# Eight column groups instead of six in the k-blocked opening of a two-layer trunk, and two groups of branch B and C moved in the order

## The chip, the core and the metric

The kernel runs on one core of one Trainium2 chip. The metric is device time in microseconds (us) for one execution of the whole program, both layers. The core has a matmul engine (PE, with its weight loads shown as PEld), a vector engine (DVE), a scalar engine (ACT), GpSimd (POOL) and SyncE (SP), which here issues most of the DMA transfers.

## The reference

384 tokens (128 of a prompt and 256 of a latent grid) of width 2048 go through two layers. Each layer is one input projection, three branches side by side, one output projection and a layer norm:

```
u    = x * (1 + scale) + shift                 # scale, shift, gate = silu(c) @ w_ada + b_ada
proj = u @ w_in                                # 2048 -> 8976 columns, float32
A: RWKV-7 scan, both directions, 8 heads x 64  (conv of r, k, v; decay and a from a LoRA; gate)
B: mLSTM, both directions, 4 heads x 128       (conv of q, k; v, o, i, f; gate)
C: differential attention, 8 heads             (q, k, v; gate)
x    = layer_norm(ALPHA * x + gate * (concat(A, B, C) @ w_out))
```

`w_in` is 2048 x 8976 and `w_ada` 2048 x 6144 for each layer. Context keys, values and final states of the prompt are outputs too.

## The kernel before

**Products.** Every float32 operand of the projections is split in two parts, `hi` (by ACT) and `lo` (by DVE, one in four by POOL). A product of 128 rows of k, 128 columns and 384 tokens is three matmuls. The 16 tiles of k, the two halves of 256 columns and the three matmuls make 96 matmuls for a *column group*, the unit of the order below.

**The opening.** A layer's first groups can't wait for all of `u`. `gemm_head` takes `GROUPS[l]` column groups by blocks of k: in the first layer there are `BLOCKS[0] = 8` blocks of two k tiles. For each block and group it makes 12 matmuls, and the partial result goes from PSUM into an SBUF tile (`part`): ACT copies it in block 0, DVE adds it (`add`) in blocks 1 to 7. After the last block a group's own evacuation runs (for branch A's r, k and v: a convolution, `a_rkv`). The tiles are borrowed from tags that branch A uses later (`HEAD`). In the first layer the same stretch also makes scale and shift: `first0` strews the loads and small matmuls of `w_ada` (eight loads of 512 KB for each block) among the groups, and turns `x` round on PE. Order of the groups: LoRA, k (two groups), r (two), v (first); the second v group follows as an ordinary group (`gemm_ch`, loads of 512 KB, the sum stays in PSUM).

**The main part.** `layer_plan` writes the order of the groups out by hand: after the opening the rest of v, then for C's pairs of heads v, q, k and a gate (`c_pair`, `c_gate`), then `MIX` (a letter for each group: c for C's last v, q and k; q for B's query and key groups; v for B's value groups), then B's gates, C's last gate, A's gates, and the output projection. Branches are generators ("streams"): between two chunks of dense matmuls `pump` lets a few segments of the ready streams in, by a planner's own clocks. So dense groups are the cover under which the thin, chained work of the branches runs. Where an order demands that a branch be over, `drain` writes out all that is left of it with no dense work between:

- `b_first` (before B's first q group) drains A's front stage "AF", since `QK` takes the tile `big0` that it reads.
- `to_b` (before B's first v group) drains all of A and "post"; `a_end` is A's last part (group norm, then the bonus term).
- `c_qk` drains the pair of C heads before, when the next pair's q is evacuated (`self.drain(f"C{h // 2 - 1}")`).
- `b_start` (after B's last v group) starts `b_main`. Its heads wait until all eight q and k tiles are there (`bqk < 8`).
- `o_rest` (after six loads of the output projection) drains everything.

The order is fixed when the program is built; each engine then works through its own list in order.

Of the kernel before, what the change touches and what calls it, by code (L numbers as in the profile page):

```python
# [21 lines left out]
T = 384  # L22
# [11 lines left out]
O_CQ, O_CK, O_CV, O_CGATE = 4880, 5904, 6928, 7952  # L34
# [3 lines left out]
RAWB = 3  # L38
CUTB = 4
LOADS = 6  # L40
GROUPS = (6, 6)
TWO = 100.0, 0.0
ADA = ((0.0, 1.0), (0.0, 1.0))
WARM, DENSE = 3100.0, 2.0
# [5 lines left out]
CPOOL = 4  # L50
PESHARE = 2000.0, 2000.0
HEAD = ("PG", 2), ("QHt", 2), ("Tt", 2), ("BK", 1), ("QH", 1), ("UV", 1), ("ce00", 1), ("ce10", 1)
MIX = "cccqqqvvvvq", "cccqqqvvvvq"
PRIO = {"E": -1, "R": 0, "N": 0, "U": -1, "X": 0, "C": 0, "A": 0, "AI": 0, "AF": 0}
AHEAD = 700.0, 500.0
LAT = 130.0
# [146 lines left out]
class Hybrid:  # L203
# [604 lines left out]
    def gemm_head(self, wv, groups, nb):  # L808

        part = {}  # L810
        bk, hb = KT // nb, KB // 2

        def place():
            for tag, n in HEAD + ((("ce01", 1), ("ce11", 1)) if self.first else (("GE", 2),)):
                for _ in range(n):
                    t = self.ct([128, T], tag) if tag[0] == "c" else self.mt([128, T], tag, bufs=2 if n > 1 else 1)
                    part[len(part) // 2, len(part) % 2] = t

        def add(g, j, kb, o, evac):
            t = part[g, j]  # L820
            if kb == 0:
                self.nc.scalar.copy(t, o)
                return
            self.nc.vector.tensor_tensor(t, o, t, OP.add)
            if kb == nb - 1:
                yield
                yield from evac(j, t)

        def chunk(g, kb, h, hv, lv, evac):
            if g == kb == h == 0:  # L830
                place()
            if h == 0:
                part["ps"] = [self.acc() for _ in range(2)]
            for kk in range(hb):
                kt = kb * bk + h * hb + kk
                self.need_u(kt)
                st, sp = (h == 0 and kk == 0), (h * hb + kk == bk - 1)
                for j in range(2):
                    c = slice(j * 128, j * 128 + 128)
                    o = part["ps"][j][:, 0:T]  # L840
                    self.nc.tensor.matmul(o, hv[:, kk, c], self.uh[:, kt, :], start=st, stop=False)
                    self.nc.tensor.matmul(o, hv[:, kk, c], self.ul[:, kt, :], start=False, stop=False)
                    self.nc.tensor.matmul(o, lv[:, kk, c], self.uh[:, kt, :], start=False, stop=sp)
                    if sp:
                        self.evacuate(add(g, j, kb, o, evac), part["ps"][j])
                self.pump()

        return [[Step("w", lambda h, hv, lv, g=g, kb=kb, evac=evac: chunk(g, kb, h, hv, lv, evac),
                      lambda kb=kb, c0=c0: wv()[:, kb * bk:kb * bk + bk, c0:c0 + 256], 256, bk // hb)
                 for g, (c0, evac) in enumerate(groups)] for kb in range(nb)]  # L850
# [875 lines left out]
    def layer_plan(self, l, first):  # L1726
# [14 lines left out]
        def ch(c0, f, i0, *korder):  # L1741
            return self.gemm_ch(wi, c0, lambda j, s: f(i0 + j, s), *korder)

        cols = [(O_LORA, self.a_lora, 0)] + [(128 * i, self.a_rkv, i) for i in (4, 6, 0, 2, 8, 10)]
        n = GROUPS[l]
        gemm = self.gemm_head(wi, [(c0, lambda j, s, f=f, i=i: f(i + j, s)) for c0, f, i in cols[:n]], BLOCKS[l])
        head = first(gemm, call(begin))
        main = sum((ch(*x) for x in cols[n:]), [])
        self.nhead = n
        v0 = self.gemm_t(wi, O_CV, 256, lambda tb, s: self.c_v(0, tb, s))  # L1750
        main += v0
# [1 line left out]
        def c_pair(pr):  # L1753
            return [self.gemm_t(wi, O_CV + 256 * pr, 256, lambda tb, s: self.c_v(pr, tb, s)),
                    ch(O_CQ + 256 * pr, lambda h, s: self.c_qk(h, 0, s), 2 * pr),
                    ch(O_CK + 256 * pr, lambda h, s: self.c_qk(h, 1, s), 2 * pr) + call(self.c_start, pr)]

        for pr in range(3):
            main += sum(c_pair(pr)[1 if pr == 0 else 0:], []) + ch(O_CGATE + 256 * pr, self.c_gate, 2 * pr)

        def to_b():
            self.drain("A", "post")
# [6 lines left out]
        vs = [self.gemm_t(wi, O_BV + 260 * g, 260, lambda tb, s, g=g: self.b_vo(g, tb, s)) for g in range(4)]  # L1769
        vs[0][0:0] = call(to_b)  # L1770
        vs[3] += call(b_start)
        qs = [ch(O_BQK + 128 * i, self.b_qk, i) for i in range(0, 8, 2)]
        qs[0][0:0] = call(self.b_first)
        parts = {"c": c_pair(3), "v": vs, "q": qs}
        for x in MIX[l]:
            main += parts[x].pop(0)
        for p in (0, 2):
            main += ch(O_BGATE + 128 * p, self.b_gate, p)
        main += ch(O_CGATE + 256 * 3, self.c_gate, 6)
        korder = (2, 0, 3, 1)  # L1780
        for p in (0, 2):
            main += ch(O_AGATE + 128 * p, self.a_gate, p, (0, 1, 2, 3) if p == 0 else korder)
# [8 lines left out]
        else:  # L1791
# [18 lines left out]
            main = main[:at] + tail  # L1810
# [10 lines left out]
        n = sum(1 for st in main if st.kind == "w") - 32  # L1821
# [183 lines left out]
    def run(self):  # L2005
# [51 lines left out]
        plan = self.layer_plan(0, first0)  # L2057
        self.early = 64 + BLOCKS[0] * GROUPS[0] - GROUPS[0]
        for l in range(1, DEPTH):
# [39 lines left out]
```

## Time and profile before

| | |
|---|---|
| median of 3 runs | 2265.77 us (2263.94 to 2270.36) |
| the profiled execution, its own time | 2266.75 us |
| span of its trace | 2265.0 us |
| PE busy | 2160.2 us (95%) |
| mean granted clock of PE | 0.979 |

The profile is of one execution. Its own time is 1.75 us more than its span (what lies before the first and after the last instruction), and 0.98 us more than the median. A clock of 1.00 is 2.4 GHz, 0.50 is 1.2 GHz. Every instruction bears line 156, that of the helper which records it, so rows are told apart by their tiles: `acc` is the PSUM of the projections, `ada` that of `w_ada`, `mx` that of the branches; `cq` and `ck` are C's queries and keys, `big` is `big0` and its kind. Ends of matmuls are modelled, so a matmul that is listed with 0.34 us may start 0.18 us behind the one before.

### The profile page before, as it was taken

The numbers are of one execution on the slowest core, as the hardware profiler recorded it, in microseconds if no ns is written. First come the engines' busy times: TensorE is split into PE (matmuls) and PEld (weight loads), VectorE is DVE, ScalarE is ACT, GpSimd is POOL, SyncE is SP. The second block draws the span as 40 slices with busy tenths as digits, with TensorE's granted clock in tenths as the row PEclk, the third lists the DMA queues.
The fourth block names the chain that finished last, engine by engine and source line by source line (L and its number), as shares of the span: only waits on it lengthen the run. The fifth ranks groups of instructions, "written<-read, shape, count | busy, mean of one in ns | idle before, by whom it ended". The sixth has DMA issues, their size and how long they took to land.

```text
span 2265.0 us, 45639 instructions
## 1 busy us (share of the span) xinstructions
PE 2160.2 (95%) x17629; PEld 1903.1 (84%) x17629; DVE 1409.5 (62%) x3792; ACT 950.1 (42%) x2207; POOL 664.6 (29%) x894
## 2 busy tenths in 40 slices
PE   5999999999999999999998999999989999999998
PEld 3778878777787888889998998788878888999997
DVE  1667776766765633577338677777676754367634
ACT  2345344343343433444327443434334443344543
POOL 3111333423332211112436123352433320111344
PEclk9999999999999999999999999999999998999998
DMA  9995433433434465544465432232222323434444
GB/s 317 314 317 145 148 114 106 120 105 108 129 115 126 151 186 162 168 145 150 152 219 176 127 115 76 83 97 82 82 82 78 92 86 113 122 103 120 144 142 144
DMA packets 313794, 314.90 MB, mean 139 GB/s; under 512 B 17569, under 2 KB 309030, under 8 KB 313450
## 3 DMA queue, kind: packets, MB, share of 16 engines
q1 hardware_dynamic: 305450, 299.49, 43.5%
q0 software_dynamic: 3616, 10.22, 1.3%
q8 instruction: 139, 2.28, 0.4%
q10 hardware_dynamic: 4512, 2.28, 0.3%
q14 instruction: 77, 0.63, 0.1%
HBM read 298.83 MB, written 13.12 MB: 138 GB/s over the span
## 4 chain that ended last, share of the span: by engine, by line
PE 69%; DVE 15%; DMA 5%; ACT 4%; issue 4%; POOL 2%; SPq 1%; DVEq 0%; ACTq 0%; POOLq 0%
PE acc L156 50%; PE mx L156 16%; DMA raw<-in_w_in_dram 3%; PE ada L156 3%; DVE lo L156 3%; ACT hi L156 2%; DVE mixed L156 2%; DVE big L156 1%; DVE GE L156 1%; POOL crs L156 1%; DVE tm L156 1%; POOL lo L156 1%; DVE BK L156 1%; DVE cmx L156 1%; DVE Di L156 1%
## 5 line engine op out<-in xcount | busy, mean ns | idle before, releaser
L156 PE MATMUL acc<-uh,hi 128*128 128x384 f32 x2240 | 809.1, 361 | 14.1 <-ACT hi L156 7.4
L156 PE MATMUL acc<-uh,lo 128*128 128x384 f32 x2240 | 763.4, 341 | 2.3 <-DVE lo L156 0.8
L156 PE MATMUL acc<-ul,hi 128*128 128x384 f32 x2240 | 762.9, 341 | 1.7 <-DVE ul L156 1.7
L156 DVE TENSOR_TENSOR lo<-raw,hi 128x512 fp32r<-128x512 f32 (+1 forms) x496 | 361.3, 739 | 494.7 <-ACT hi L156 478.0
L156 ACT CAST hi<-raw 128x512 fp32r<-128x512 f32 (+1 forms) x659 | 395.6, 619 | 427.0 <-PE acc L156 274.0
L156 POOL TENSOR_TENSOR lo<-raw,hi 128x512 fp32r<-128x512 f32 (+1 forms) x163 | 222.6, 1366 | 998.3 <-ACT hi L156 914.4
L156 PEld LDWEIGHTS acc<-uh,hi 128*128 128x128 f32 x2240 | 426.5, 190 | 75.9 <-issue 29.7
L156 PEld LDWEIGHTS acc<-ul,hi 128*128 128x128 f32 x2240 | 426.6, 190 | 6.1 <-DVE ul L156 3.3
L156 PEld LDWEIGHTS acc<-uh,lo 128*128 128x128 f32 x2240 | 425.2, 190 | 6.9 <-DVE lo L156 5.5
L156 PE MATMUL acc<-hi,uh 128*128 128x256 f32 (+1 forms) x768 | 227.8, 297 | 4.0 <-DVE mixed L156 1.7
L156 PE MATMUL acc<-lo,uh 128*128 128x256 f32 (+1 forms) x768 | 218.0, 284 | 1.1 <-DVE lo L156 1.0
L156 PE MATMUL acc<-hi,ul 128*128 128x256 f32 (+1 forms) x768 | 217.1, 283 | 0.0
L156 PEld LDWEIGHTS acc<-hi,uh 128*128 128x128 f32 x768 | 145.8, 190 | 22.8 <-issue 12.3
L156 PEld LDWEIGHTS acc<-lo,uh 128*128 128x128 f32 x768 | 145.9, 190 | 2.3 <-DVE lo L156 2.3
L156 PEld LDWEIGHTS acc<-hi,ul 128*128 128x128 f32 x768 | 145.9, 190 | 0.0
L156 ACT ACTIVATE ce<-mx,cmx 128x384 f32<-128x384 f32 (+1 forms) x96 | 48.0, 505 | 109.0 <-DVE cmx L156 109.0
L156 PE MATMUL ada<-raw,sil 128*32 128x256 f32 x1088 | 87.9, 398 | 4.3 <-DMA raw<-in_w_ada_dram 4.3
L156 ACT COPY mixed<-mx 64x256 f32<-64x256 f32 x120 | 44.0, 366 | 101.8 <-PE mx L156 99.9
L156 PEld LDWEIGHTS mx<-mixed 128*64 128x64 f32 x1536 | 54.1, 141 | 24.8 <-issue 9.1
L156 PE MATMUL mx<-mixed 128*64 128x64 f32 x1536 | 67.5, 232 | 3.7 <-DVE mixed L156 2.4
L156 DVE TENSOR_TENSOR mixed<-mx,mixed 128x256 f32<-128x256 f32 (+1 forms) x96 | 40.1, 418 | 34.3 <-PE mx L156 33.9
L156 POOL TENSOR_TENSOR GE<-th,big 64x512 f32<-64x512 f32 x24 | 33.0, 1375 | 81.6 <-PE mx L156 69.6
(449 smaller groups left out, 3074.2 us busy)
## 6 DMA issues: line engine op xcount, KB each, us to landing
raw<-in_w_in_dram SPq DMA_DIRECT2D x224, 512.0 KB
raw<-in_w_ada_dram SPq DMA_DIRECT2D x136, 512.0 KB
raw<-in_w_out_dram SPq DMA_DIRECT2D x64, 512.0 KB
big<-in_w_ada_dram SPq DMA_DIRECT2D x42, 512.0 KB
raw<-in_w_in_dram SPq DMA_DIRECT2D x32, 520.0 KB
GE<-in_w_ada_dram SPq DMA_DIRECT2D x14, 512.0 KB
cq<-xs SPq DMA_DIRECT2D x32, 192.0 KB
big<-in_w_in_dram SPq DMA_DIRECT2D x21, 256.0 KB
```

Source lines behind the costliest of these rows:

```text
L156: r = f(*args, **kw)
```

## The change

The first layer's opening takes eight groups: the second v group of A and C's third gate (`c_gate` of heads 4 and 5) come in, with four more SBUF tiles (`hx`). Both then leave the main part of the first layer. In both layers B's fourth q group moves from behind B's v groups to before them, and C's last gate moves from behind B's gates to right behind B's v groups. The last block's order of groups is LoRA, k, k, r, r, v, v, gate.

```
-GROUPS = (6, 6)
+GROUPS = (8, 6)
-MIX = "cccqqqvvvvq", "cccqqqvvvvq"
+MIX = "cccqqqqvvvvg", "cccqqqqvvvvg"
...
-            for tag, n in HEAD + ((("ce01", 1), ("ce11", 1)) if self.first else (("GE", 2),)):
+            for tag, n in HEAD + ((("ce01", 1), ("ce11", 1), ("hx", 4)) if self.first else (("GE", 2),)):
                 for _ in range(n):
-                    t = self.ct([128, T], tag) if tag[0] == "c" else self.mt([128, T], tag, bufs=2 if n > 1 else 1)
+                    t = self.ct([128, T], tag) if tag[0] == "c" else self.mt([128, T], tag, bufs=n)
...
+        cols += [(O_CGATE + 512, self.c_gate, 4)]
...
-        main = sum((ch(*x) for x in cols[n:]), [])
+        main = sum((ch(*x) for x in cols[n:7]), [])
...
-            main += sum(c_pair(pr)[1 if pr == 0 else 0:], []) + ch(O_CGATE + 256 * pr, self.c_gate, 2 * pr)
+            main += sum(c_pair(pr)[1 if pr == 0 else 0:], [])
+            if pr < 2 or n < 8:
+                main += ch(O_CGATE + 256 * pr, self.c_gate, 2 * pr)
...
-        parts = {"c": c_pair(3), "v": vs, "q": qs}
+        parts = {"c": c_pair(3), "v": vs, "q": qs, "g": [ch(O_CGATE + 256 * 3, self.c_gate, 6)]}
...
-        main += ch(O_CGATE + 256 * 3, self.c_gate, 6)
```

Counted in dense groups, the order of the first layer is then: after the opening 1 + 3 + 4 + 3 + 3 = 14 groups up to `b_first` (16 before), four more up to `to_b` (three before), so 18 in place of 19 between the opening and `to_b`. In the second layer it is 16 up to `b_first` as before, and 20 in place of 19 up to `to_b`. In both layers five groups follow `b_start` before the output projection, where there were six.

## Rows read from the trace of the kernel before

**Rows 1.** The page: busy time of the engines, share of the span, instructions.
```profile
PE 2160.2 (95%) x17629; PEld 1903.1 (84%) x17629; DVE 1409.5 (62%) x3792; ACT 950.1 (42%) x2207; POOL 664.6 (29%) x894
```

**Rows 2.** Windows over the opening: us; PE, PEld, DVE, ACT, POOL busy; PEclk; DMA; GB/s.
```profile
30.00:40.00 10.00, 6.54 (x38) 4.89 (x40) 3.09 (x6) 4.08 (x9) 1.38 (x3) 0.69 1.08 363
40.00:50.00 10.00, 8.92 (x85) 5.84 (x80) 3.24 (x7) 4.66 (x11) 1.28 (x1) 0.97 1.01 336
50.00:60.00 10.00, 9.39 (x73) 6.98 (x70) 3.91 (x8) 7.68 (x17) 1.28 (x1) 1.00 0.95 318
...
170.00:180.00 10.00, 10.00 (x59) 10.00 (x58) 8.83 (x19) 6.04 (x11) 3.49 (x5) 1.00 0.67 185
180.00:190.00 10.00, 7.94 (x31) 6.37 (x29) 8.56 (x20) 4.25 (x8) 0.76 (x2) 0.83 0.37 109
...
60.00:160.00 100.00, 100.00 (x766) 77.32 (x759) 63.36 (x144) 37.42 (x75) 15.95 (x18) 1.00 0.97 324
```

**Rows 3.** Timeline of PE in the opening: start us, us, operation, count, idle before.
```profile
99.18 0.34 PE L156 MATMUL acc<-uh,hi 128*128 128x384 f32 x1
...
100.59 0.34 PE L156 MATMUL acc<-uh,lo 128*128 128x384 f32 x1
100.86 0.64 PE L156 MATMUL ada<-big,sil 128*32 128x256 f32 x8
101.43 0.44 PE L156 MATMUL acc<-uh,hi 128*128 128x384 f32 x1
```

**Rows 4.** Timeline of PE at the opening's end.
```profile
183.43 1.11 PE L156 MATMUL mx<-gt,const 128*128 128x384 f32 x2 [1.25 <-ACT gt L156]
```

**Rows 5.** Timeline of PE at the end of branch A, second layer.
```profile
1875.50 0.91 PE L156 MATMUL mx<-PG,const 128*128 128x384 f32 x2
1880.19 0.33 PE L156 MATMUL mx<-q,big 64*64 64x64 f32 x2 [3.78 <-DVE q L156]
```

**Rows 6.** Windows there, columns as in rows 2.
```profile
1875.00:1880.00 5.00, 1.41 (x10) 0.38 (x10) 4.86 (x13) 3.23 (x6) 1.28 (x1) 1.00 0.59 159
1880.00:1885.00 5.00, 4.12 (x36) 3.60 (x36) 2.98 (x9) 4.85 (x7) 0.00 (x0) 0.54 0.17 58
1885.00:1890.00 5.00, 4.99 (x58) 4.99 (x59) 4.63 (x8) 0.00 (x0) 0.00 (x0) 0.50 0.00 0
1890.00:1895.00 5.00, 5.00 (x29) 4.88 (x28) 1.57 (x5) 0.50 (x1) 0.00 (x0) 0.59 0.35 105
```

**Rows 7.** Timeline of PE at the end of branch A, first layer.
```profile
734.65 0.91 PE L156 MATMUL mx<-PG,const 128*128 128x384 f32 x2
...
779.13 0.33 PE L156 MATMUL mx<-q,big 64*64 64x64 f32 x2
```

**Rows 8.** Timeline of ACT around C's third pair, first layer.
```profile
586.97 0.29 ACT L156 COPY ck<-acc 128x128 f32<-128x128 f32 x1
...
686.52 0.37 ACT L156 COPY rraw<-acc 128x256 f32<-128x256 f32 x1 [3.82 <-PE acc L156]
```

**Rows 9.** Timeline of PE there.
```profile
668.88 1.03 PE L156 MATMUL mx<-const,cq 128*128 128x128 f32 x3 [1.03 <-POOL cq L156]
...
677.82 1.00 PE L156 MATMUL mx<-const,QH 64*128 64x64 f32 x8
```

**Rows 10.** Timeline of PE in branch B, first layer, then second.
```profile
902.62 0.53 PE L156 MATMUL mx<-const,PG 4*128 4x4 f32 x6
...
918.83 0.71 PE L156 MATMUL mx<-const,big 128*128 128x128 f32 x3
...
1065.15 0.49 PE L156 MATMUL mx<-const,big 128*128 128x128 f32 x3
...
1981.66 0.53 PE L156 MATMUL mx<-const,PG 4*128 4x4 f32 x6
...
1994.86 0.75 PE L156 MATMUL mx<-const,big 128*128 128x128 f32 x4
...
2121.82 0.49 PE L156 MATMUL mx<-const,big 128*128 128x128 f32 x3
```

## The prediction, made before the changed kernel was run

> **What bounds the kernel now.** I read the page first: PE is busy for 95% of the span, PE's weight loads for 84%, and no other engine for more than 62% [rows 1]. The change removes no matmul and adds none. So it can only win back time in which PE waits or runs at its lower clock (2266.75 us hold about 105 us of idle PE, 2265.0 less 2160.2), or lose some. The question is where that time lies, and whether a place that the change touches has it.
>
> Next I read windows over the opening, where DMA is busiest: there one would look for a PE that starves. PE is short of work up to about 60 us: idle 3.46 us from 30 to 40, 1.08 from 40 to 50, 0.61 from 50 to 60. From 60 to 160 us it is busy 100.00 of 100 us, with DMA at 0.97 [rows 2]. Since busy time is modelled, I checked with PE's timeline that no wait hides in it: nine products in a row start within 1.41 us of each other, 0.176 us apart, the `ada` matmuls of a load follow 0.27 us behind the last of them, and the next product starts 0.57 us later, with no wait named [rows 3]. Both resources are near full here, and PE is the one that has no gap. At the opening's end PE is idle for 2.06 us, most of it in a wait of 1.25 us for ACT's `gt`, which stands behind a queue of convolutions, and its clock falls to 0.83 for 10 us [rows 2, 4].
>
> Then I went through PE's timeline for waits over 3 us in the places where the order changes. One stands out: in the second layer `a_end` is not over when `to_b` drains it. The last matmul on `PG` starts at 1875.50, and the next one 4.69 us later, having waited 3.78 us for DVE; the bonus matmuls follow bare, at a clock of 0.54, 0.50 and 0.59 [rows 5, 6]. The same piece of the first layer (from the `PG` matmul at 734.65 to the last `q` at 779.13) runs under dense groups without a wait [rows 7].
>
> **The opening, its size.** Two groups of eight blocks move in. A block of a group is 12 matmuls at 0.176 us [rows 3], 2.11 us; 7 blocks x 2 x 2.11 = 29.6 us of PE work before the last block and 4.2 us in it, all of which leaves the main part. Where PE is already full this is neutral: same work, other place. It only pays where PE waits for lack of work after the first product could start. That is 40 to 60 us: 1.08 + 0.61 = 1.69 us at most [rows 2]; the 3.46 us before it lie ahead of the first product, which the number of groups does not touch. I take 1 us of gain, bounds 0 and 1.7.
>
> The extra evacuations are 28 adds of DVE and four copies of ACT; by the nearest rows DVE has 63.36 of 100 us busy and ACT 37.42 [rows 2]. At some 0.5 us each that is 14 us of DVE over 150 us, hidden by PE; without that cover it would cost at most those 14 us. The weights come in loads of 256 KB and not 512 KB, the same bytes: eight more issues on SP, hidden while SP issues ahead.
>
> The Trainium skill would read this stretch otherwise: its page "Perfetto Trace Analysis", section "Identifying the Most-Contended Engine", calls matmul busy time a poor measure of headroom and wants the share of weight-load time. By that the opening has 22.7 us free in 100 (PEld 77.32), where the pure product stretch from 170 to 180 has none (10.00 of 10) [rows 2]. I side with the start-to-start times [rows 3], in which `ada` matmuls load few columns; what the other reading would give is the first rival.
>
> **The opening's end.** DVE and ACT get two more value tiles to convolve and two gates in the same queue, but PE gets 4.2 us more in the last block and the wait for `gt` comes from the k tiles, which stand ahead. The second pair of value tiles shares two `rraw` buffers with the first, so PE may have to turn the first round while DVE is late; behind those matmuls stands C's first v group. Bounds: minus 3.8 us (the 2.06 us and 10 x 0.17 of clock gone) and plus 3.8 (the same again) [rows 2, 4]. I take +1.
>
> **The first layer beside C and A.** With the third gate gone, C's next q group ends two groups after the third pair starts, not three. The pair's keys are there at 586.97, the next q is evacuated at 686.52; the pair's last transposes run at 668.88, 82 us after its keys [rows 8, 9]. Two groups are then some two thirds of the 99.6 us, 66 us: some 15 us of the pair's chain would still be open when `c_qk` drains it. Its remaining steps are short ones that other streams hold apart now; bare they cost less, perhaps a third. Behind the drain stand the last matmuls of that q group and all of PE. I take +3, bounds 0 and 8. A's front ends at 677.82 [rows 9]; the longer opening shifts it by about 30 us, close under the point where `b_first` drains it. +1, bounds 0 and 6. A's own end keeps room: its first-layer end has 45 us in which the second layer takes 15 [rows 5, 6, 7].
>
> **The second layer's `to_b`.** The fourth q group now stands between `a_end` and the drain: 96 x 0.176 = 16.9 us of dense work over a chain that runs bare from 1875.5 to about 1890, where 58 short matmuls in 5 us give way to 29 long ones: 14.5 us [rows 5, 6]. What can go: the waits, 5 - 1.41 + 5 - 4.12 = 4.5 us, and the lower clock, 5 x (0.46 + 0.50 + 0.41) = 6.9 us [rows 6]: 11.3 us. `pump` lets A's steps in by its own clocks, and the first layer took 45 us for them under cover [rows 7], so a remnant may still be drained: I take -9, bounds -11.3 and -3. The group's four loads pass the sixteen of B's v groups on SP, with DMA at 0.59 and less there, so none should be late; its two convolutions join DVE's list, which is busy for 4.86 of 5 us at the stall [rows 6] and is one more reason not to take the whole 11.3. What is late next is nothing but PE: B's value products follow.
>
> **Branch B.** It loses one group of cover (16.9 us) between `b_start` and the output projection, and gains an earlier start: its heads wait for the last q now, from 902.62 to 918.83 in the first layer and from 1981.66 to 1994.86 in the second (16.2 and 13.2 us) [rows 10]. These nearly cancel. The heads end at 1065.15 and 2121.82 [rows 10], close to `o_rest`. C's last gate only changes its place. +2 for both layers, bounds 0 and 10.
>
> **Sum**: -1 + 1 + 3 + 1 - 9 + 2 = -3 us. Against the profiled execution, 2266.75 - 3 = 2263.75; the median stands 0.98 lower, so 2262.8, rounded to 2263.
>
> **Rivals.** (a) The loads bound the opening. For it: DMA at 0.97, PEld at 77.32 of 100 [rows 2]; against it: no gap in PE's starts [rows 3]. Then two groups cost only their bytes there, 14 x 262144 bytes at 324 GB/s = 11.3 us in place of 29.6: 18.3 us more gain, less the 1 us already taken, about 2245.5.
> (b) The cover in the first layer suffices everywhere and the second layer's drain vanishes whole: -1 - 11.3 = -12.3, about 2253.5. For it: C's and A's chains speed up when fewer other streams compete; against it: the first layer's 82 us for a pair.
> (c) The other side: B's heads need their number of dense groups, not their time. For it: both layers spend the same five groups and six loads on them, though the first takes 146.3 us and the second 127.0 [rows 10]. Then one group's worth of B stands bare in each layer, up to 33.8 us in all; half of that, 17 us, with the other terms at -5 gives +12, 2278. It turns the sign once the bare part exceeds 5 us, and is slower by 0.3% from 12 us on.
> (d) The drain in the second layer stays bare, because `pump` holds A's last steps back: -9 becomes 0, about 2272. The headline's "beside branch A" is half true in any case: C's last gate stands behind `to_b`.
>
> **How the numbers follow.** Forecast 0.48 (its own range 2257 to 2269), (a) 0.07, (b) 0.20, (c) 0.15, (d) 0.10. A measurement can tell about 0.3% here, 6.8 us: faster is below 2259, slower above 2272.6. Faster: all of (a), 0.19 of (b), and a quarter of the forecast, 0.12: 0.38. Slower: 0.14 of (c), 0.04 of (d): 0.18. Same: 0.44. The range reaches to (b) and to (c): 2250 to 2278, leaving out (a), the upper part of (c) and some 0.05 of the tails.
>
> **What would show it.** In the changed profile PE should be full from about 55 us to the end of the opening, which ends some 30 us later; waits of PE under 2 us at the second layer's `to_b`, and a clock of 1.00 there; a wait of some us on C's third pair at its next q; B's last transposes close to `o_rest`, with the clock at 1.00. The opening's end coming less than 25 us later would show (a). A clock at half beside B's last heads would show (c).

## The result, and the profile of the changed kernel

The changed kernel takes 2317.18 us (median of 4 runs, 2314.34 to 2320.54), the kernel before 2267.48 in the same comparison: ratio 1.0229 [1.021, 1.0249], 50 us slower. The profiled execution has 2320.54 us and a span of 2318.6, 53.6 us more than before. The forecast of 2263 and its whole range are missed on the side that had the chance 0.18.

The page's busy line, to be held against [rows 1]:

```profile
PE 2181.6 (94%) x17629; PEld 1917.6 (83%) x17629; DVE 1423.6 (61%) x3820; ACT 951.4 (41%) x2211; POOL 659.4 (28%) x894
```

The matmuls are the same 17629. PE's idle time went from 105 to 137 us (2318.6 less 2181.6), and PE is busy for 21 us longer, which is work at the lower clock (mean 0.969 and not 0.979). So of the 54 us 32 are waits of PE, and 21 are matmuls that took longer at the lower clock.

First the opening, in windows (columns as in [rows 2]):

```profile
40.00:50.00 10.00, 9.19 (x75) 6.47 (x74) 0.59 (x4) 4.15 (x9) 1.26 (x1) 1.00 0.99 320
50.00:60.00 10.00, 9.45 (x69) 7.28 (x66) 3.97 (x7) 8.22 (x19) 1.29 (x1) 1.00 0.88 280
60.00:160.00 100.00, 100.00 (x709) 77.86 (x707) 66.13 (x140) 36.24 (x71) 14.11 (x15) 1.00 0.89 285
```

PE is full from 60 us on as before, while DMA's share falls from 0.97 to 0.89: the loads did not bind. Branch A begins (DVE's memset of `LP`) at 205.22 and not 172.89 us, 32.3 us later, where two groups of seven blocks are 29.6. This part went as forecast.

Then the opening's end, the same columns, in steps of 5 us:

```profile
205.00:210.00 5.00, 5.00 (x30) 5.00 (x29) 3.48 (x9) 3.94 (x8) 0.94 (x1) 1.00 0.68 172
210.00:215.00 5.00, 3.00 (x17) 2.44 (x15) 4.38 (x11) 1.62 (x3) 0.00 (x0) 1.00 0.36 105
215.00:220.00 5.00, 3.75 (x12) 2.77 (x11) 3.96 (x9) 1.74 (x4) 2.84 (x5) 0.66 0.45 112
220.00:225.00 5.00, 4.22 (x24) 3.90 (x23) 4.03 (x10) 3.20 (x6) 0.43 (x1) 1.00 0.35 112
225.00:230.00 5.00, 2.57 (x15) 2.28 (x14) 4.82 (x13) 3.89 (x7) 0.00 (x0) 0.98 0.00 0
230.00:235.00 5.00, 1.92 (x6) 1.41 (x5) 4.86 (x13) 0.62 (x1) 2.32 (x3) 0.50 0.33 105
235.00:240.00 5.00, 4.70 (x54) 4.19 (x54) 4.82 (x13) 1.08 (x2) 0.00 (x0) 0.50 0.35 105
```

From 210 to 235 us PE has work for 15.46 of 25 us and its clock falls to 0.66 and 0.50; DVE is busy for 22.05 of the same 25. PE's timeline names what it waits for (the wait in brackets); [rows 4] is the place before:

```profile
214.46 0.91 PE L156 MATMUL mx<-gt,const 128*128 128x384 f32 x2 [2.00 <-ACT gt L156]
216.63 1.65 PE L156 MATMUL mx<-gt,const 128*128 128x384 f32 x2 [1.25 <-ACT gt L156]
...
228.67 0.41 PE L156 MATMUL acc<-uh,hi 128*128 128x384 f32 x1 [2.43 <-DVE ce L156]
235.18 1.94 PE L156 MATMUL mx<-const,rraw 128*64 128x64 f32 x24 [3.26 <-DVE rraw L156]
```

And DVE's timeline shows what stands in front of those releases:

```profile
224.84 1.65 DVE L156 SCALAR_TENSOR_TENSOR big<-BK,P,big 128x127 f32<-128x127 f32 x4
226.41 1.64 DVE L156 SCALAR_TENSOR_TENSOR big<-QH,P,big 128x127 f32<-128x127 f32 x4
227.97 1.01 DVE L156 TENSOR_TENSOR ce<-acc,ce 128x384 f32<-128x384 f32 x2
228.90 0.68 DVE L156 TENSOR_TENSOR lo<-raw,hi 128x512 fp32r<-128x512 f32 x1
229.50 1.65 DVE L156 SCALAR_TENSOR_TENSOR big<-UV,P,big 128x127 f32<-128x127 f32 x4
231.06 1.65 DVE L156 SCALAR_TENSOR_TENSOR big<-ce,P,big 128x127 f32<-128x127 f32 x4
232.63 0.55 DVE L156 TENSOR_TENSOR ce<-acc,ce 128x384 f32<-128x384 f32 x1
```

Each k or r tile leaves four convolution instructions, 1.65 us, in DVE's list (the outer taps of its convolution); the adds that free PE's accumulators, and the `lo` parts of the next operands, stand behind them.

The kernel before has the same taps at that place, and DVE is as full: 14.57 of the 15 us from 190 to 205. But PE is full there too, 14.69 of 15. It works off the second value group, whose 96 matmuls lie between 190.18 and 213.4 us; the transposes that read `rraw` come after most of them and do not wait:

```profile
190.00:195.00 5.00, 4.94 (x33) 4.31 (x32) 4.86 (x11) 3.37 (x6) 1.29 (x1) 1.00 0.07 10
195.00:200.00 5.00, 5.00 (x37) 4.32 (x32) 4.82 (x14) 2.45 (x4) 0.00 (x0) 1.00 0.67 203
200.00:205.00 5.00, 4.75 (x25) 3.76 (x22) 4.89 (x12) 0.99 (x2) 0.00 (x0) 1.00 0.60 186
```

```profile
206.34 1.62 PE L156 MATMUL mx<-const,rraw 128*64 128x64 f32 x48
```

In the changed kernel that group's products are spread over the eight blocks, and the transposes at 235.18 stand right behind the last one.

Now the later places. A's end in the second layer, PE's timeline and windows (before: [rows 5, 6]):

```profile
1948.45 0.33 PE L156 MATMUL mx<-q,big 64*64 64x64 f32 x2 [2.24 <-DVE mixed L156]
...
1951.35 0.47 PE L156 MATMUL mx<-q,big 64*64 64x64 f32 x2 [1.34 <-DVE mixed L156]
```

```profile
1945.00:1950.00 5.00, 2.76 (x51) 2.50 (x47) 4.73 (x11) 1.09 (x3) 0.00 (x0) 1.00 0.00 0
1950.00:1955.00 5.00, 3.66 (x38) 3.54 (x38) 4.55 (x9) 0.00 (x0) 0.00 (x0) 0.51 0.02 3
```

The stall that was to go is still there. B's end, PE's timeline in the first and second layer and the windows around the second (before: the last rows of [rows 10], without a wait):

```profile
1100.40 0.99 PE L156 MATMUL mx<-const,big 128*128 128x128 f32 x3 [3.40 <-DVE big L156]
...
2181.61 0.99 PE L156 MATMUL mx<-const,big 128*128 128x128 f32 x3 [6.02 <-DVE big L156]
```

```profile
2175.00:2180.00 5.00, 0.59 (x5) 0.18 (x3) 4.59 (x19) 0.52 (x2) 0.00 (x0) 0.88 0.67 210
2180.00:2185.00 5.00, 3.39 (x12) 3.24 (x13) 3.13 (x11) 2.00 (x4) 1.10 (x1) 0.50 0.00 1
```

PE waits for B's last heads in both layers now. C's third pair and A's front, ACT's and PE's timelines (before: [rows 8, 9]):

```profile
683.15 0.37 ACT L156 COPY rraw<-acc 128x256 f32<-128x256 f32 x1 [1.25 <-PE acc L156]
```

```profile
683.66 0.60 PE L156 MATMUL mx<-const,cq 128*128 128x128 f32 x3
...
723.38 0.69 PE L156 MATMUL mx<-const,QH 64*128 64x64 f32 x4 [0.86 <-ACT ce L156]
```

The pair ends as the next q is evacuated, with PE full (5.00 of 5 us from 680 to 685). A's front ends 45.6 us later than before, in the drain of `b_first`, in thin windows:

```profile
710.00:715.00 5.00, 3.24 (x34) 2.96 (x34) 2.63 (x6) 2.48 (x7) 0.78 (x2) 1.00 0.34 110
715.00:720.00 5.00, 4.09 (x54) 2.87 (x52) 4.86 (x18) 0.82 (x4) 2.87 (x4) 1.00 0.09 28
720.00:725.00 5.00, 3.18 (x30) 2.60 (x28) 3.36 (x14) 2.57 (x12) 0.73 (x1) 0.63 0.32 75
```

**A table by stages** helps to read all runs. The windows view gives for each stage its length, PE's busy time and the granted clock; the loss is length less busy, plus length x (1 - clock). The clock has two digits, so a stage of 470 us is known to 2 us only, and the sums are no exact account of the spans. The opening's end reaches from DVE's memset of `LP` to PE's first `LP` matmul. The stages after it end with C's last key, with the first transfer behind A's drain, 6 us before B's first matmul on its i and f, 2 us after the start of B's last transposes, and with the output projection. The ranges are over the profiles of eight programs with six groups and seven with eight, all from the experiments below; each was profiled once. The run without the taps of k and r (e13) is left out of them.

| loss, us | before | changed | six groups, mean (range) | eight groups, mean (range) |
|---|---|---|---|---|
| opening, to A's begin | 26.7 | 25.1 | 23.9 (19.5 to 28.5) | 25.3 (23.4 to 27.9) |
| **opening's end** | 3.9 | 16.4 | 4.1 (3.9 to 4.5) | 16.7 (15.4 to 17.3) |
| layer 1, to C's last key | 28.6 | 39.1 | 30.7 (27.3 to 33.6) | 37.0 (34.6 to 39.1) |
| layer 1, to the end of A's drain | 0.2 | 9.7 | 0.3 (0.1 to 1.1) | 8.0 (0.4 to 19.9) |
| layer 1, B's values | 2.7 | 4.7 | 3.4 (1.8 to 6.9) | 3.0 (1.4 to 6.8) |
| layer 1, B | 7.0 | 12.1 | 6.1 (3.5 to 12.1) | 9.0 (6.5 to 17.5) |
| layer 1, output | 11.7 | 18.1 | 13.5 (9.6 to 17.9) | 16.6 (13.8 to 19.0) |
| layer 2, to C's last key | 39.1 | 45.3 | 37.7 (32.4 to 45.2) | 36.4 (27.6 to 45.3) |
| layer 2, to the end of A's drain | 12.5 | 12.2 | 7.0 (0.0 to 12.5) | 9.4 (2.3 to 12.2) |
| layer 2, B's values | 2.1 | 1.4 | 1.1 (0.0 to 2.1) | 1.3 (0.0 to 2.1) |
| layer 2, B | 1.2 | 10.0 | 3.1 (0.8 to 8.3) | 7.8 (1.2 to 10.0) |
| layer 2, output | 19.2 | 20.0 | 19.2 (17.0 to 20.7) | 19.9 (19.3 to 20.3) |

### The profile page after: what moved, and what is told of

It is laid out like the page before. It is cut to its first block, busy times and chain, and to the rows that moved or that the text cites. A ratio compares the mean times of both kernels' runs of the same rounds, so it can differ in the third digit from the quotient of the medians.

```text
span 2318.6 us, 45678 instructions
## 1 busy us (share of the span) xinstructions
PE 2181.6 (94%) x17629; PEld 1917.6 (83%) x17629; DVE 1423.6 (61%) x3820; ACT 951.4 (41%) x2211; POOL 659.4 (28%) x894
## 4 chain that ended last, share of the span: by engine, by line
PE 64%; DVE 17%; DMA 7%; ACT 4%; issue 4%; POOL 3%; SPq 1%; DVEq 0%; ACTq 0%; POOLq 0%
PE acc L156 47%; PE mx L156 15%; DMA raw<-in_w_in_dram 5%; DVE lo L156 3%; PE ada L156 3%; DVE mixed L156 2%; ACT hi L156 2%; DVE big L156 1%; POOL lo L156 1%; DVE tm L156 1%; DVE GE L156 1%; DVE cmx L156 1%; ACT ce L156 1%; DVE Di L156 1%; POOL crs L156 1%
## 5 line engine op out<-in xcount | busy, mean ns | idle before, releaser
L156 POOL TENSOR_TENSOR lo<-raw,hi 128x512 fp32r<-128x512 f32 (+1 forms) x162 | 215.2, 1328 | 1034.3 <-ACT hi L156 968.6
L156 PEld LDWEIGHTS acc<-hi,uh 128*128 128x128 f32 x768 | 146.3, 191 | 23.5 <-issue 12.1
```

Source lines behind the costliest of these rows:

```text
L156: r = f(*args, **kw)
```

## The experiments

Every ratio is against runs of the kernel before on the same chip, taken beside it. In the first four expectations theory 1 is that the losses of cover add up, and theory 2 that the new order alone does it. From the fifth on theory 1 is still cover, theory 2 the evacuation queue at the opening's end, and theory 3 the planner's draw.

**Taking the change apart.** Four kernels: the new order with six groups; eight groups in the old order (C's last gate back behind B's gates); only the q group moved; seven groups in the old order.

```
e1:  GROUPS = (6, 6)   MIX = "cccqqqqvvvvg", ...
e2:  GROUPS = (8, 6)   MIX = "cccqqqvvvvq", ...
e3:  GROUPS = (6, 6)   MIX = "cccqqqqvvvv", ...
e4:  GROUPS = (7, 6)   MIX = "cccqqqvvvvq", ...
```

> Six groups in the opening as before, with the new order in both layers (B's fourth q group before its v groups, C's last gate right behind them). Theory 1, every part takes cover away from a branch and the losses add: only branch B loses here, its heads are drained at the end of their cover in both layers, 12 to 18 us above the kernel before, ratio 1.005 to 1.008. Theory 2, the order alone does most of it: 35 us or more, ratio above 1.015. My prediction's own sum for these terms was minus 7 us, ratio 0.997.

> Eight groups in the opening of the first layer, with B's fourth q group and C's last gate where they were. Theory 1: the crowded end of the opening costs some 12 us, branch A's shorter cover 20 to 30 us more, since here two groups fewer stand before the drain of A: 30 to 45 us above the kernel before, ratio 1.013 to 1.020. Theory 2: 15 us or less, ratio under 1.007. The second layer should be as before within 5 us.

> Six groups; only B's fourth q group moves before the v groups, C's last gate stays behind B's gates. Theory 1: the cover of B has the same count of groups as with the gate moved too, so the time is that of the order alone within 5 us. Rival: the gate's place is what costs, and this one is within 3 us of the kernel before.

> Seven groups in the opening (the second v group of A joins, C's third gate does not), old order. Theory 1, the end of the opening is crowded by the v tiles on DVE: PE idle and slow clock there as with eight groups within 4 us, and one group of cover less for A: 12 to 25 us above the kernel before. Rival, the gate group's place (two groups between C's third pair and the next q) costs most of the first layer's loss: under 10 us here.

Order alone 1.0004 [0.9983, 1.0026]; eight groups alone 1.0186 [1.0154, 1.0219]; q alone 1.0006 [0.9988, 1.0024]; seven groups 1.0095 [1.0065, 1.0124]. So the groups moved into the opening cost most of the time, and the new order by itself costs nothing that shows; the loss that I expected of it did not come.

The order's parts are to be seen in the stages. With the new order and six groups, A's drain in the second layer loses 3.1 us (0.0 with q alone) where the kernel before loses 12.5: the forecast gain is there. But B loses 8.3 in the same layer where the kernel before loses 1.2. PE's waits there, from 2080 to 2130 us of the run with the new order:

```profile
PE mx L156 <- DVE big L156: 6.0, 1, 6.0
```

It is the wait of the changed kernel at 2181.61. With eight groups and the old order, B in the second layer loses 1.2 us, and the drain 11.5. So with both moves B pays where A gains. With the q group alone B loses only 2.8 us there, with the same five groups behind `b_start`; all nine programs with C's last gate in its new place lose 8.1 to 10.0. So in the second layer most of B's loss goes with the gate's place and not with the number of groups.

**Cover for A's end, and other numbers of groups.** In the first and fourth kernel A's drain goes behind three quarters of B's first value group; in the second the seventh group of the opening is the gate, and the second value group stays an ordinary one; the third has five groups.

```
-        vs[0][0:0] = call(to_b)
+        vs[0][3:3] = call(to_b)                 # e5: before, e8: the changed kernel
...
+        cols.insert(6 if n == 7 else 7, (O_CGATE + 512, self.c_gate, 4))     # e6
-GROUPS = (6, 6)
+GROUPS = (5, 6)                                  # e7
```

> The kernel before, with the drain of branch A put before the last quarter of B's first value group instead of ahead of it, in both layers: A's end gets three quarters of a dense group more cover, and nothing else moves. Theory 1 (cover is what the kernel is short of; every dense group that stands before branch A begins is lost to the branches): the second layer's bare end of A, 14.5 us long, is mostly covered, the first layer has nothing to win: 4 to 9 us faster, 2258 to 2264. Theory 2 (the value tiles' evacuation at the opening's end is what costs): the same few us or nothing, it says nothing on this place. If the wait stays as it is in the second layer, A's last steps are held back by the planner's clocks and not by the place of the drain: 2267.

> Seven groups in the first layer's opening in the old order, but the seventh is C's third gate and not the second value group of A, which stays an ordinary group. Theory 1 (cover): what kind of group moves is no matter, about 21 us slower as with the value group: 2283 to 2291. Theory 2 (the evacuation of a second pair of value tiles at the opening's end): two gates have no convolution and no guarded tile, so the opening's end loses 4 us as before, and the whole is 2267 to 2275. Between: the opening's end gives 8 us back and the rest stays, about 2279.

> Five groups in the first layer's opening, old order: A's first value group becomes an ordinary one behind the opening. Theory 1 (cover), if it holds on this side too: 21 us back, less what PE now waits in the opening. Five groups have 14.8 us less of PE's work before the last block; the loads lose 1.8 MB, 5.7 us at 324 GB/s, so 6 to 9 us of idle PE: 2252 to 2259. If six groups already leave the branches all the cover that they can use, only the loss in the opening stays: 2272 to 2277, and the price of a seventh and eighth group is a threshold, not a slope.

> The changed kernel, with the drain of branch A put before the last quarter of B's first value group. Theory 1 (cover): the first layer loses 9.8 us from C's third key group to the drain and the second 12 there; three quarters of a group should give 5 to 13 us back: 2304 to 2312. Theory 2 (the opening's end): 2317, unchanged within 3 us.

Late drain in the kernel before: 0.9995 [0.9978, 1.0011]. The drain in the second layer loses 4.0 us and not 12.5, but the time is the same: a miss. Gate as the seventh: 1.006 [1.0041, 1.0078], opening's end 7.1 us; with the value group as the seventh it was 14.8. So the value group as the seventh costs 11 us there, and the gate, which leaves the value group standing behind the last block, 3. Five groups: 1.0085 [1.0056, 1.0114]. A's begin comes 14.3 us earlier, as the work says, and PE's idle time in the opening grew by 1 us only, so the loads did not bind here either; still 17 us are lost, more than I gave it by any theory, 3 of them at the opening's end and 8 at A's drain. Why the opening's end loses 7.2 us there, with still more dense work behind it, is open: PE's only named waits in it are two for ACT's `gt`, 3.7 us together. With the rest of the kernel as it is, six is the best of five to eight. Late drain in the changed kernel: 1.0123 [1.0094, 1.0151], some 24 us better than the changed kernel, more than expected. Only part of that lies where the edit is: the second layer up to C's last key, which it does not touch, loses 27.6 us and not 45.3. That raised the third theory.

**The planner's draw.** No group moves. The planner's clocks start 1.137 or 2.275 us later, which draws the places of the thin segments anew.

```
-        self.clk = {"PE": 0.0, "DVE": 0.0, "ACT": 0.0, "POOL": 0.0, "DMA": 0.0}
-        self.clk["SP"] = 0.0
+        self.clk = {"PE": 1137.0, "DVE": 1137.0, "ACT": 1137.0, "POOL": 1137.0, "DMA": 1137.0}
+        self.clk["SP"] = 1137.0                  # p1; 2275.0 in p2
```

> The kernel before, with all of the planner's clocks started at 1137 ns in place of 0, a third of the window in which it counts columns. No group moves; only the places at which the planner lets thin segments in are drawn anew. Theory 1 (cover, and the opening's end): within 0.3% of before. Theory 3 (the draw itself is worth as much as the change): 10 to 30 us slower or faster.

> The same with 2275 ns, two thirds of the window. Theory 1: within 0.3% of before. Theory 3: 10 to 30 us away from before.

> The changed kernel with the planner's clocks started at 1137 ns. Theory 1 (cover and the opening's end): slower than before by 1.5 to 2.5%, as the changed kernel. Theory 3 (a bad draw): a good part of the 50 us is gone, under 1% slower. From the stages of the runs so far I expect a share of each: some 12 us at the opening's end and 20 of cover in the first layer stay, and what the second layer lost up to the start of B (from 38 us in one run with the same order there to 60) changes with the draw: 1.3 to 2.2%.

> The same with 2275 ns. Theory 1: 1.5 to 2.5% slower than before. Theory 3: under 1%. Mixed: 1.3 to 2.2%, and the opening's end loses 14 to 18 us of idle time and clock whatever the draw, where the kernel before loses 4.

Before: 1.001 [0.9994, 1.0027] and 0.9986 [0.9972, 1.0001]. Changed: 1.0163 [1.0136, 1.0191] and 1.0114 [1.0089, 1.0139], against 1.0229 with clocks from zero. The draw is worth up to 1.15% in the changed kernel, so up to half of its loss is the draw, and half stays with any of the three. What changes is A's drain in the first layer: it loses 1.0 and 0.4 us in these two, where the changed kernel loses 9.7, though the order is the same. With 2275 ns the second layer's drain loses 3.2 and not 12.2 us. What does not change is the opening's end: 17.3 and 17.1 us.

**What sets the opening's end.** Seven groups as in e4 with four `rraw` tiles; the changed kernel without the outer taps of value tiles 10 and 11; then without those of the k and r tiles. Beside them the changed kernel with C's last gate before B's values in the first layer, and the new order with six groups and the late drain.

```
-"rraw", bufs=2
+"rraw", bufs=4                                   # e9, with ("hx", 2)
...
-        for t0, t1 in SEG:
+        for t0, t1 in () if self.first and b == "cab" and i >= 10 else SEG:   # e11; i < 8 in e13
...
-MIX = "cccqqqqvvvvg", "cccqqqqvvvvg"
+MIX = "cccqqqqgvvvv", "cccqqqqvvvvg"             # e10
```

> Seven groups as in the run with the second value group alone, but four tiles rraw in place of two, so that the second pair of value tiles need not wait until the first pair is turned. Theory 2a (the shared tiles make PE wait at the opening's end): the wait of 4.3 us for rraw goes and most of the 14.8 us of idle time and clock there, down to 5 to 8. Theory 2b (DVE's and ACT's list is full there, and the stretch lasts as long as that list, 49 us, whatever PE has to do): it loses 12 to 15 us still, and the whole stays at 0.7 to 1.2% slower than before.

> The changed kernel without the two outer taps of the convolution of value tiles 10 and 11 in the first layer (left out: that part of the values). It takes 8 of DVE's instructions, 3.2 us, out of the opening's end. Theory 2b (DVE's list sets the stretch): 3 to 6 us less lost there, of 16.4. Theory 1 (missing dense work alone): no less than 15. The whole is drawn anew by the planner, so I read the stretch and not the total: anything from 1.0 to 2.3% slower than before.

> The changed kernel with C's last gate really beside branch A in the first layer: ahead of B's first value group and its drain, so that 19 dense groups stand between the opening and the drain, as in the kernel before. Theory 1 (cover): what the first layer loses between C's last keys and the end of A's drain falls from 14 us to under 5; B's end has one group less behind its start and loses 5 us more: 1.2 to 2.2% slower than before. Theory 2: no change outside the draw, and the opening's end loses its 14 to 18 us as ever.

> Six groups, the change's order in both layers, and the drain of A before the last quarter of B's first value group: the two moves that each left the time as it was, together. If the second layer's bare end of A is all that is to be won, it is gone (0 to 3 us lost there in place of 12) and B's end pays 7: 0.996 to 1.000 of before.

Four tiles: 1.0021 [1.0002, 1.004]. The opening's end still loses 12.0 us. PE's waits there:

```profile
PE acc L156 <- DVE ce L156: 5.5, 2, 3.1
PE mx L156 <- ACT gt L156: 2.8, 2, 2.2
```

The wait for `rraw` is gone and another one on the same DVE list has grown in its place, as theory 2b said, though the whole came out under its 0.7%. Without the taps of tiles 10 and 11: 1.0211 [1.0181, 1.0242], opening's end 16.4 us, the same waits: those taps stand at the end of DVE's list, behind everything that PE waits for. So neither the fall that theory 2a expected of the four tiles nor the one that 2b expected of these taps came.

Gate before B's values: 1.0254 [1.022, 1.0288]. A's drain loses 8.6 us, hardly less than 9.7, and B 17.5 where it lost 12.1, so the group handed from B to A cost B 5 us and gave A 1. Order and late drain together: 1.0041 [1.0025, 1.0058], no better than either alone. The drain still loses 7.6 us and the stage before it 45.

The last two: the taps of k and r, and the four tiles in the kernel before as a candidate that might beat both.

> The changed kernel without the two outer taps of the convolution of A's k and r tiles in the first layer (left out: that part of r and k). It takes 32 instructions of DVE, 8 times 1.65 us or 13.2 us, out of the list between the last block's adds; the taps of tiles 10 and 11, which the earlier run left out, stood behind them. Theory 2b (DVE's list between the adds keeps PE's accumulators and the next operands back): the opening's end loses under 9 us of idle time and clock, of 16.4 in the changed kernel, and the waits for ce and rraw (2.4 and 3.3 us) shrink. Theory 1 (the dense group that used to stand there is missing, whatever DVE does): 14 us or more. I read the stretch; the whole is drawn anew, 1.0 to 2.2% slower than before.

> The kernel before with four tiles rraw in place of two: a candidate that may beat both, since the run with seven groups gained 17 us by that step. If the guard on the two tiles makes the planner finish streams early all through the branches, it gains here too, 5 to 15 us: 0.993 to 0.998. If that gain was the planner's draw, 0.998 to 1.003.

Without the taps of k and r: 1.0119 [1.01, 1.0139]. The windows at the opening's end:

```profile
210.00:215.00 5.00, 5.00 (x42) 3.90 (x39) 3.96 (x8) 4.39 (x10) 0.00 (x0) 1.00 0.65 195
215.00:220.00 5.00, 5.00 (x28) 4.62 (x27) 2.42 (x5) 4.97 (x7) 0.57 (x1) 1.00 0.05 18
220.00:225.00 5.00, 4.57 (x25) 3.97 (x23) 3.86 (x9) 3.50 (x7) 2.72 (x5) 1.00 0.48 145
225.00:230.00 5.00, 4.04 (x61) 3.48 (x62) 4.89 (x10) 2.44 (x6) 1.89 (x3) 1.00 0.22 76
230.00:235.00 5.00, 5.00 (x82) 4.39 (x80) 4.67 (x12) 4.14 (x9) 0.00 (x0) 1.00 0.35 108
```

PE has work for 23.61 of the 25 us in which it had 15.46, and the clock stays at 1.00. The stretch lasts 32.7 us and not 50.9, and loses 1.4. It also holds fewer matmuls (289 and not 332), since the planner places some of them later, so the same 55 us from A's begin are the fairer measure: kernel before, changed kernel, without the taps of k and r.

```profile
173.00:228.00 55.00, 52.63 (x431) 45.81 (x430) 41.67 (x92) 30.95 (x53) 7.89 (x10) 0.97 0.50 144
205.00:260.00 55.00, 45.15 (x369) 39.25 (x368) 38.81 (x89) 28.12 (x48) 6.83 (x10) 0.88 0.33 94
205.00:260.00 55.00, 53.34 (x478) 46.48 (x477) 40.17 (x79) 32.85 (x61) 14.83 (x17) 1.00 0.44 134
```

By length less busy, plus length x (1 - clock), they lose 4.0, 16.5 and 1.7 us. The planner's draw does not do that: the seven other programs with eight groups lose 15.4 to 17.3 at the opening's end. So DVE's 13.2 us of taps between the adds of the last block hold PE there. Four tiles in the kernel before: 0.9991 [0.9976, 1.0005], so four tiles by themselves gain nothing. The good time of the seven-group run with four tiles came in large part from stages that the edit does not aim at (in the second layer 33.7 and not 45.1 us up to C's last key, 10.5 and not 16.9 at A's drain); that this was its draw is likely and not shown. No version beat the kernel before by more than its interval.

## Why the prediction was wrong

**The step that failed** is the opening's end, and under it the sentence that moving the groups is neutral, "same work, other place". I priced the place that the groups went to, not the one that they left. The second value group had stood right behind the last block: 16.9 us in which PE needs nothing from DVE but operands, while DVE works off the taps of k and r. What stands of it in the last block now is 2.1 us of products (4.2 with the gate's) that themselves want adds. The stretch stays about as long, 50.9 us and 48.9 before, and PE has less to do in it; without the 13.2 us of taps the loss is gone, so DVE's list sets it. I took +1 us with bounds of 3.8 either way, and the upper bound was no more than the lower one with its sign turned. It is +12.5 in the profile, and the ranges over all runs with six and with eight groups do not touch (3.9 to 4.5 and 15.4 to 17.3). I had named the shared `rraw` tiles; they were a small part, as the run with four tiles shows (12.0 us lost and not 14.8). I had gone by the average of DVE over the opening (63.36 of 100 us) and passed over the rows of its end, which have DVE at 8.83 and 8.56 of 10 [rows 2]; in the changed kernel it is at 4.0 to 4.9 of 5 there. This step is 12.5 of the 53.6 us; the other terms follow.

**The cover in the first layer.** The mechanism was there, but its size was not one number. A's front in `b_first` was +1 with bounds up to 6. The three thin windows from 710 to 725 us hold 4.5 us of idle PE and 1.9 of clock, as much as the upper bound, though not all of it is A's front. A's own end I had put at nothing ("keeps room"); the stage with the drain lost 9.5 us more, and 0.4 and 1.0 in all with two other draws of the same order, so there the draw decides.

C's third pair was +3 with bounds 0 and 8. The stage up to C's last key lost 10.5 us more (6.3 in the means), and most of it lies where the gate left, between C's third keys and its last ones. The same windows, kernel before and changed kernel:

```profile
586.97:716.06 129.09, 125.18 (x1306) 104.58 (x1302) 82.55 (x256) 51.35 (x144) 40.55 (x66) 1.00 0.40 120
610.04:715.09 105.05, 97.75 (x941) 82.36 (x942) 73.10 (x205) 42.20 (x123) 39.33 (x65) 0.95 0.40 118
```

That is a loss of 3.9 and of 12.6 us. The nine programs that have the gate in the opening lose 8.4 to 15.9 us there, among them the one with the gate as its seventh group (10.6); the eleven that have it in its old place lose 1.7 to 7.3. So the term stood in the right place and was too small. The mechanism that I gave, the drain of the third pair, is not shown: the pair's end has no wait, and the waits of PE that are named there have several sources (2.8 us for a transfer of cached keys, 2.2 and 1.9 for DVE).

**The second layer's drain** was -9. With six groups it came: 12.5 us fell to 3.1 and 0.0. In the changed kernel it did not (12.2), and with a later planner's clock it did (3.2). So rival (d) came true here, and since a shift of the planner's clocks alone undoes it, that `pump` decides is shown; it holds for some draws only.

**Branch B** was +2 for both layers with bounds 0 to 10. It lost 5.1 and 8.8 us more, 14 together, near the 17 us of rival (c), and the sign named for it is there (a clock of 0.50 beside B's last heads, 2180 to 2185 us). In the second layer this is no matter of draw alone: 8.3 us in the run with the order alone, 2.8 with the q group alone, 0.8 to 1.3 with the old order. So I had looked at the wrong move: C's last gate, which I said "only changes its place", brings most of it, and why its place matters is open. With the order alone the drain's gain of 9 and B's loss of 7 nearly cancel, but that does not explain the 1.0004: with the q group alone the two places lose 11 us less than before, and the time is the same (1.0006). Other stages took that back, the first layer's output projection for one (17.9 and 11.7 us), and no run says why.

**Right** were the opening's own size (the stage loses 25.1 us where it lost 26.7; -1 was forecast, though the stage differs by 9 us among the programs with six groups, so the last microsecond is luck) and that the loads don't bind, against rival (a): A's begin moved by 32.3 us. The share of weight-load time, one of the two measures of headroom that the Trainium skill names (page "Perfetto Trace Analysis", section "Identifying the Most-Contended Engine"), does not agree with this trace: PEld is at 77.86 of 100 there, and the two groups still took their whole 29.6 us.

**What is open.** Beyond the opening's end (12.5 us), the stretch that C's third gate left (8.7), the first layer's drain (9.5) and B (14), the changed kernel lost 6.4 us in the first layer's output projection and 6 in the second layer up to C's last key. Programs with six groups reach the same losses in both stages (17.9 and 45.2 us), so the draw can explain them, and no run isolates them. Why B loses when C's last gate moves is open too.

## What to carry to other kernels

When dense work is moved to a place where the matmul engine is already full, price the place that it leaves: look for the engine whose list the dense work was covering there, by windows of a few microseconds and not by the mean of the stage. When a planner draws the order of small pieces, shift its phase once or twice in both kernels before reading a difference of 1%; here the same order gave 1.0114 to 1.0229. And look at what the giver loses when a group of cover is handed from one branch to the next; here B lost 5 us where A got 1.

## What was not expected of the hardware

The kernel before had medians of 2267.36 us on the chip of the first four experiments and 2259.49 to 2261.51 on four other chips, 0.3% apart, as much as the effects that were looked for. A change of a program is read only beside runs on the same chip.
